# A gated recurrent stage: elementwise work moved off GpSimd, time-reversed value tiles moved one by one, and filling work re-spaced

## The chip, the cores and the metric

The kernel runs on one core of a Trainium2 chip. The core has TensorE (matrix products, PE in the profile), VectorE (DVE), ScalarE (ACT), GpSimd (POOL) and SyncE (SP, which only issues transfers), and 16 DMA engines. Each engine works through its own instructions strictly in order and waits on semaphores for the others. The metric is device microseconds of one execution; lower is better.

## The reference

One block of a hybrid model, batch 1, 1024 tokens, width 1024, fp32:

```python
h = rms_norm(x, norm1_gain)
hq, hf, hi, hg, sq, sk, sv, ga, gb = split_cols(h @ w_in, ...)
o_hg = hgrn2_mixer(hq, hf, hi, lower_bounds)              # recurrent stage, 8 heads of 128
o_hg = rms_norm(o_hg, hg_out_norm) * sigmoid(hg)
o_sb = stick_breaking(rms_norm(sq), rms_norm(sk), sv)     # attention stage, 16 heads of 64
x = x + (sigmoid(ga) * (o_hg @ w_hg_out) + sigmoid(gb) * (o_sb @ w_sb_out)) @ w_o
gate, up = split_cols(rms_norm(x, norm2_gain) @ w_ffn_in, ...)
x = x + (silu(gate) * up) @ w_ffn_out
```

The mixer works in chunks of 64 tokens. With `f = lb + (1 - lb) * sigmoid(hf)`, `k = 1 - f` and `c` the running sum of `log f` in the chunk:

```python
scores = einsum('td,tsd,sd->ts', q, exp(c[t] - c[s]) masked to s <= t, k)
o = scores @ v + (q * exp(c)) @ state
state = exp(c[last]) * state + (k * exp(c[last] - c)).T @ v
```

## The kernel before, in words

**Stages.** The order is: norm and transpose of x; projections of the forget and output gates of all heads (put into DRAM as `d_f` and `d_g`); the recurrent stage, head by head, some 190 to 555 us into the profile; the attention stage; the output projections; the feed-forward layer. Products of fp32 are made of three passes on a high part and a rest (`mm3`, lines 231 to 233). TensorE's order is exactly the order of the program text. The other engines' orders, and those of the DMA queues, are chosen by a scheduler from the program's order and its own idea of when each instruction is ready.

**Layout of a head.** Tokens lie in eight tiles of 128. Of each pair of tiles, the keys of the second are stored in reversed token order (`by_tile`, `odd`), so that a mask on scores can be shared; the values `v` of these tiles (index 1, 3, 5, 7) have to be reversed along their rows too. `hg_v` computes `v` for two heads at once (a pair of heads h, h + 1, h even), two token tiles per step `tp`. Line 560 copies the first of the two straight into `v`; line 557 copies the second into `vs`, which line 558 stores to DRAM (`d_v`). `turn_v` (line 564) then copies the whole pair's `d_v` with reversed rows to `d_vr` by a DMA issued from ScalarE's queue; `load_v` (line 568) loads `d_vr` into `v`, one DMA for each head of the pair, also from ScalarE's queue. For h > 0 the turn stands at the start of the pair's first `prep`, the load in its first step.

**A head's work.** `hg_gates(h)` makes `kv = 1 - f` and the running sum `c`. `prep` makes decayed keys and queries (`kb`, `qb`, `ke`, `qe`): subtraction, exponential on ScalarE, product. The tile of scores `sc` is cleared on GpSimd for every head. Then come 15 own steps: `base(0)` and `base(1)` (scores within 4 tokens, written into `sc` under a mask), `across` (scores between the halves of a tile), four `level`s (scores between blocks of 32, 16, 8 and 4 tokens; `level_prep` makes their operands), `turn` (transpose of `ke`, copied to `ket` by ScalarE, line 658), `state` (`ket` times `v`, line 667), `read` (`sc` times `v` and state times `qe`, lines 715 and 717) and `norm`. The first `state` step reads the token tiles 0 to 3, the second 4 to 6; tile 7 is read by `read(1)` alone. Of the operand buffers, `kb`, `qb` and the four levels' `kq` share four slots, and `ke`, `qe` and `sc` have one each; `kb`, `qb` and `ke` for the next head are made while this one runs.

**What stands on GpSimd.** `kv` (line 585), the clearing of `sc` (600), the subtraction for `qb` (604), for `ke` (614), the query half of `level_prep` (687), the last product of `norm` (729), and the DMAs that make the rest of a weight by accumulation (`rest_by_dma`, line 125).

**Filling.** Between own steps `weave` puts steps of other products: for head h the projection of q for head h + 1 (16 steps of three matmuls with 512 columns), then half of the `v` of a pair (32 steps of three matmuls with 256 columns); for heads 6 and 7 gate projections instead. Each own step has a number, each filling step too; after each own step, filling is put until

```python
pump(lead + (total - lead) * acc / span)
```

is reached, where `acc` is the sum of the own numbers so far and `span` their total. The numbers are weights for the order alone. An even head h also carries the first half of the v of pair h + 2, an odd head the second half of the v of pair h + 1.

**SyncE's queue** carries the weight loads (`wr`, line 136, two buffers), the loads of `fv` and `sg`, the stores of `d_v` and those of the head's output `d_ohg`. The program asks for them at the head's start in this order: the weights of the filling (`load_blocks`), then `prep`, then `hg_load` of the next head.

Of the kernel before, what the change touches and what calls it, by code (L numbers as in the profile page):

```python
# [7 lines left out]
F32 = mybir.dt.float32  # L8
# [3 lines left out]
AF = mybir.ActivationFunctionType  # L12
ALU = mybir.AluOpType
# [3 lines left out]
P = 128  # L17
S = 1024
D = 1024
KT = D // P  # L20
HS = 512
NT = S // P
# [19 lines left out]
def hybrid_block(ctx, tc, x, norm1_gain, w_in, lb_logits, hg_out_norm, sb_q_norm, sb_k_norm,  # L42
# [506 lines left out]
    def hg_v(h, tiles=range(4), get=None):  # L549
        get = get or in_block(2048 + h * P, 256)  # L550

        def evac(tp, ps):
            if tp == 0:
                for j in range(2):
                    hd[h + j]["v"] = hg.tile([P, NT, P], F32, tag="v", bufs=4, name="v")
            vs = hg.tile([P, 2 * P], F32, tag="vs", name="vs")
            nc.scalar.copy(vs, ps[:, 2 * P:])
            nc.sync.dma_start(d_v[h // 2, tp], vs)
            for j in range(2):
                nc.scalar.copy(hd[h + j]["v"][:, 2 * tp, :], ps[:, j * P:(j + 1) * P])  # L560
        return proj_v(get, evac, tiles)

    def turn_v(h):
        nc.scalar.dma_start(d_vr[h // 2], d_v[h // 2, :, ::-1, :])

    def load_v(h):
        for j in range(2):
            nc.scalar.dma_start(hd[h + j]["v"][:, 1::2, :],
                                d_vr[h // 2, :, :, j * P:(j + 1) * P].rearrange("a p c -> p a c"))

# [9 lines left out]
    def hg_gates(h):  # L580
        d = hd[h]
        fv = d["fv"]
        kv = d["kv"] = hg.tile([P, S], F32, tag="kv", name="kv")
        for dst, src in by_tile(kv, fv):
            nc.gpsimd.tensor_scalar(dst, src, -1.0, 1.0, op0=ALU.mult, op1=ALU.add)
        c = d["c"] = hg.tile([P, S], F32, tag="c", name="c")
        order(nc.scalar.activation(c, fv, AF.Ln, bias=tiny), *last["tables"])
        nc.vector.tensor_tensor_scan(c, rmask, c, initial=0.0, op0=ALU.mult, op1=ALU.add)

    def hg_head(h):  # L590
# [5 lines left out]
        def prep():  # L596
            if h % 2 == 0 and h > 0:
                turn_v(h)
            sc = e["sc"] = hg.tile([P, S], F32, tag="sc", bufs=1, name="sc")
            nc.gpsimd.memset(sc, 0.0)  # L600
            kb = e["kb"] = hg.tile([P, S], F32, tag="kl", bufs=4, name="kb")
            qb = e["qb"] = hg.tile([P, S], F32, tag="kl", bufs=4, name="qb")
            c4 = c.rearrange("p (b l) -> p b l", l=4)
            nc.gpsimd.tensor_sub(qb.rearrange("p (b l) -> p b l", l=4), c4,
                                 c4[:, :, 1:2].broadcast_to([P, S // 4, 4]))
# [6 lines left out]
            for dst, src in by_tile(ke, c):  # L612
                dst, src = (a.rearrange("p a (n c) -> p a n c", c=CH) for a in (dst, src))
                nc.gpsimd.tensor_sub(dst, src[:, :, :, CH - 1:CH].broadcast_to([P, NT // 2, 2, CH]), src)
            nc.scalar.activation(ke, ke, AF.Exp)
# [61 lines left out]
        def level_prep(li):  # L677
# [6 lines left out]
            for w, dst in enumerate(halves):  # L684
                src = pairs(c)[:, :, w, :].rearrange("p a (b two l) -> p a b two l", two=2, l=L)[:, :, :, 0, :]
                nc.vector.tensor_sub(dst, src[:, :, :, L - 1:L].broadcast_to([P, NT // 2, P // (2 * L), L]), src)
            nc.gpsimd.tensor_sub(qr, cl[:, :, 1, :], cl[:, :, 0, L - 1:L].broadcast_to([P, HS // L, L]))
            nc.scalar.activation(kq, kq, AF.Exp)
# [33 lines left out]
        def norm(half):  # L722
# [5 lines left out]
            nc.vector.scalar_tensor_tensor(r, po, cols[:, 32 + h:33 + h], r, op0=ALU.mult, op1=ALU.mult)  # L728
            nc.gpsimd.tensor_mul(r, r, sg[:, sl])
            nc.sync.dma_start(d_ohg[h][:, sl], r)  # L730

        return prep, [
            (0.86, lambda: (base(0), load_v(h) if h % 2 == 0 else None, level_prep(0),)),
            (2.46, lambda: (base(1), level_prep(1),)),
            (5.60, lambda: (across(), level_prep(2),)),
            (2.24, lambda: (level(0), level_prep(3),)),
            (0.50, lambda: (turn(0),)),
            (0.80, lambda: (turn(1),)),
            (0.85, lambda: (level(1),)),
            (1.85, lambda: (state(0),)),  # L740
            (0.70, lambda: (state(1),)),
            (0.61, lambda: (level(2),)),
            (3.99, lambda: (level(3),)),
            (1.60, lambda: (read(0),)),
            (4.50, lambda: (read(1),)),
            (2.97, lambda: (norm(0),)),
            (0.45, lambda: (norm(1),)),
        ]

# [52 lines left out]
    for n in range(n0):  # L802
        if n == n0 - 5:
            get = in_block(2048, 256)
            get()
            v0 = [hg_v(0, tiles, get) for tiles in ((0, 1), (2, 3))]
        weave([], pairs0.steps(n))
        if h_sums:
            h_sums.pop(0)()
    s0ctx.close()  # L810
    hg = hgctx.enter_context(tc.tile_pool(name="hg", bufs=2, reuse_waits="tile"))
    last["tables"] = [exp_ln_tables(last["sig0"])]
    hg_load(0)
# [4 lines left out]
    weave([], v0[1])  # L818
    turn_v(0)
    def urgent(steps):  # L820
# [5 lines left out]
    for h in range(NH):  # L826
# [12 lines left out]
        if h < NH - 1:  # L839
            hg_load(h + 1)  # L840
        weave(own, fill, lead=5.53)
    hgctx.close()
# [688 lines left out]
```

## Time and profile before

| | us |
|---|---|
| median of 3 runs (lowest, highest) | 2054.48 (2050.78, 2055.08) |
| the profiled execution: its own time | 2053.37 |
| the profiled execution: span from first to last instruction | 2051.3 |
| TensorE busy | 2006.9 |
| VectorE busy | 1522.5 |
| ScalarE busy | 1141.7 |
| GpSimd busy | 318.4 |
| `d_vr<-d_v`, share of the chain of waits over the whole span | 3% |

A row of a group reads: line, engine, operation, output <- inputs, shape, count, then busy us and mean ns of one, then the engine's idle time just before these instructions and what ended it. A row of a timeline gives start and length in us, with the idle time ahead of it and its releaser in brackets; "ACTq" and "SPq" are the issue of a DMA by that queue. A row of a table by stretch gives the stretch, its length, the busy time of PE, PEld, DVE, ACT and POOL with their counts of instructions, then the clock granted to TensorE as a share of full speed, the DMA engines' busy share and GB/s. A busy TensorE is not one at its peak, since the ends of matmuls are modelled and a lower clock lengthens them.

### The profile page before, as it was taken

What the parts mean: (1) busy time and instruction counts of PE and PEld (TensorE: products, weight loads), DVE (VectorE), ACT (ScalarE), POOL (GpSimd) and SP (SyncE); (2) the same over time, 40 slices, a digit from 0 to 9 for tenths busy, and PEclk for the clock granted to TensorE, in tenths of its full rate; (3) what the DMA queues carried; (4) which work ended last, traced back from release to release, by engine and by line L of the source; (5) the groups of instructions that cost most, each with busy time, mean ns of one, the idle gap of its engine ahead of it and who ended that gap; (6) DMA issues with size and microseconds to landing.
All of it is one profiled execution on the core that took longest, in us unless ns stands there. A gap on an engine that the chain in (4) does not pass through costs nothing.

```text
span 2051.3 us, 29673 instructions
## 1 busy us (share of the span) xinstructions
PE 2006.9 (98%) x10963; PEld 1720.6 (84%) x10963; DVE 1522.5 (74%) x2355; ACT 1141.7 (56%) x1957; POOL 318.4 (16%) x431
## 2 busy tenths in 40 slices
PE   8999899999999999999999999998999999999999
PEld 8888788898888988988988888887888888888887
DVE  7853777787367877787787598999766666668975
ACT  7544464555377777777777465547433333334443
POOL 0000444444222332332231000000000000000000
PEclk9999999999999999999999999999999999999999
DMA  5234446545455445455445646413323222256131
GB/s 184 98 114 144 128 120 158 144 114 152 117 117 125 89 107 118 99 118 121 101 105 120 216 147 210 166 35 111 102 74 105 78 72 77 78 203 222 42 113 41
DMA packets 209840, 245.23 MB, mean 120 GB/s; under 512 B 12008, under 2 KB 142496, under 8 KB 209696
## 3 DMA queue, kind: packets, MB, share of 16 engines
q1 hardware_dynamic: 188928, 202.84, 31.4%
q0 software_dynamic: 13616, 35.14, 10.3%
q10 hardware_dynamic: 7152, 5.37, 0.8%
q8 instruction: 86, 1.41, 0.3%
q14 instruction: 58, 0.48, 0.1%
HBM read 146.57 MB, written 51.12 MB: 96 GB/s over the span
## 4 chain that ended last, share of the span: by engine, by line
PE 71%; DVE 9%; DMA 4%; issue 2%; ACT 2%; POOL 1%; DVEq 0%; POOLq 0%; ACTq 0%
PE pd L231 14%; PE pd L232 14%; PE pd L233 14%; DMA d_vr<-d_v 3%; PE pt L1011 3%; PE pt L233 3%; PE pt L231 3%; PE pt L232 3%; PE po L1028 2%; PE po L231 2%; PE po L1027 2%; PE po L232 2%; PE po L233 2%; PE pz L966 2%; PE pz L967 2%
## 5 line engine op out<-in xcount | busy, mean ns | idle before, releaser
L167 ACT CAST wh<-u 128x512 fp32r<-128x512 f32 (+1 forms) x280 | 183.5, 684 | 224.9 <-PE po L233 86.6
L231 PE MATMUL pd<-hT,wh 128*128 128x512 f32 (+1 forms) x716 | 286.7, 400 | 0.0
L232 PE MATMUL pd<-hT,wh 128*128 128x512 f32 (+1 forms) x716 | 276.0, 385 | 0.5 <-DVE hT L281 0.5
L233 PE MATMUL pd<-hT,wl 128*128 128x512 f32 (+1 forms) x688 | 264.9, 385 | 0.0
L231 PE MATMUL pd<-u,wh 128*128 128x512 f32 x496 | 194.0, 391 | 1.5 <-ACT c L1394 0.7
L232 PE MATMUL pd<-u,wh 128*128 128x512 f32 x496 | 193.1, 389 | 0.2 <-DVE u L168 0.2
L168 DVE TENSOR_TENSOR wl<-u,wh 128x512 fp32r<-128x512 f32 (+1 forms) x196 | 150.5, 801 | 45.7 <-ACT wh L167 43.6
L231 PE MATMUL pd<-wh,hT 128*128 128x256 f32 x512 | 153.6, 300 | 0.0
L233 PEld LDWEIGHTS pd<-hT,wl 128*128 128x128 f32 x688 | 129.2, 188 | 26.9
L978 DVE TENSOR_TENSOR_SCAN kp<-kp,dsel 128x512 f32<-128x512 f32 (+3 forms) x128 | 123.5, 965 | 37.0 <-ACT kp L971 36.4
L232 PEld LDWEIGHTS pd<-hT,wh 128*128 128x128 f32 x716 | 135.2, 189 | 18.7 <-DVE hT L281 0.9
L231 PEld LDWEIGHTS pd<-hT,wh 128*128 128x128 f32 x716 | 135.0, 189 | 18.2
L232 PE MATMUL pd<-wl,hT 128*128 128x256 f32 x512 | 145.7, 285 | 2.7 <-DMA wl<-wr 1.7
L233 PE MATMUL pd<-wh,hT 128*128 128x256 f32 x512 | 145.6, 284 | 0.0
L971 ACT ACTIVATE kp<-pz,rq 128x128 f32<-128x128 f32 (+2 forms) x192 | 114.2, 595 | 43.9 <-PE pz L967 33.2
L233 PE MATMUL pd<-u,wh 128*128 128x512 f32 x352 | 137.0, 389 | 0.0
L164 DVE TENSOR_TENSOR u<-u,u 128x512 f32<-128x512 f32 (+1 forms) x152 | 124.7, 855 | 12.3 <-DMA u<-d_ohg 7.6
L1014 DVE TENSOR_TENSOR tl<-pt,th 128x512 fp32r<-128x512 f32 (+1 forms) x160 | 100.2, 627 | 33.5 <-ACT th L1013 33.1
L985 DVE TENSOR_TENSOR a<-a,kp 128x128 f32<-128x128 f32 (+2 forms) x192 | 109.7, 571 | 17.8 <-ACT a L971 3.4
L971 ACT ACTIVATE a<-pz,rq 128x128 f32<-128x128 f32 (+2 forms) x192 | 114.3, 595 | 7.0 <-PE pt L1011 7.0
L231 PEld LDWEIGHTS pd<-u,wh 128*128 128x128 f32 x496 | 93.1, 188 | 21.6 <-ACT c L1394 1.1
L232 PEld LDWEIGHTS pd<-u,wh 128*128 128x128 f32 x496 | 93.1, 188 | 19.8 <-DVE u L168 0.5
(305 smaller groups left out, 5293.5 us busy)
## 6 DMA issues: line engine op xcount, KB each, us to landing
wr<-in_w_in SPq DMA_DIRECT2D x72, 512.0 KB, 4.0
wl<-wr POOLq DMA_DIRECT2D x59, 512.0 KB, 4.9
u<-in_w_ffn_in SPq DMA_DIRECT2D x24, 512.0 KB, 4.7
wr<-in_w_ffn_in SPq DMA_DIRECT2D x20, 512.0 KB, 4.2
u<-in_w_ffn_out SPq DMA_DIRECT2D x10, 1024.0 KB, 6.7
d_act<-c SPq DMA_DIRECT2D x33, 256.0 KB, 2.1
u<-d_act SPq DMA_DIRECT2D x8, 1024.0 KB, 5.7
qh<-qh SPq DMA_DIRECT2D x48, 128.0 KB, 2.4
```

Of the source, the lines that this page charges most:

```text
L164: e.tensor_tensor(raw(to), raw(a), raw(b), op=op)
L167: nc.scalar.copy(hi, src)
L168: e.tensor_sub(lo, src, hi.bitcast(F32))
L231: nc.tensor.matmul(ps, lh, rh, start=start, stop=False, skip_group_check=adds)
L232: nc.tensor.matmul(ps, lh, rl, start=False, stop=False, skip_group_check=adds)
L233: nc.tensor.matmul(ps, ll, rh, start=False, stop=stop, skip_group_check=adds)
L966: nc.tensor.matmul(ps[:, :n], qhi[:, qs], kk[:, k0:k0 + n], start=True, stop=False)
L971: last["sig"] = [nc.scalar.activation(t[:, 0:w], ps[:, 0:w], AF.Sigmoid, scale=rq[:, n_, col:col + 1]) for n_, t in enumerate((kp, a))]
L978: nc.vector.tensor_tensor_scan(rev, rev, dsel[:, HS - w:][:, ::-1], initial=0.0, op0=ALU.mult, op1=ALU.max)
L985: nc.vector.tensor_mul(a[:, 0:w], a[:, 0:w], kp[:, 1:w + 1])
L1011: nc.tensor.transpose(tp[:, s * P:(s + 1) * P], a[:, b * P:(b + 1) * P], ident)
L1014: nc.vector.tensor_sub(tl[:, c0:], tp[:, c0:], th[:, c0:].bitcast(F32))
```

## The change

- The subtractions for `qb`, `ke` and the query half of each level, and the last product of `norm`, are done by VectorE; `kv` is made by ScalarE as `Identity(-1 * f + 1)`. GpSimd keeps the weight DMAs.
- `sc` is one tile for the whole stage, cleared once before the first head. Every head writes the same positions of it.
- `turn_v` turns one tile step `tp` of a pair, as two halves of 128 columns: rows of 512 bytes where there were rows of 1 KB. Tile step 0, 1 and 2 are turned when the values of the next step are copied out, tile step 3 after `base(1)` of the pair's first head. All four are issued by ScalarE's queue.
- `load_v` is issued by SyncE: tile steps 0 to 2 at the start of `prep` (for head 0 after the values are done), tile step 3 after `level(1)`. For each part there is one DMA for each head of the pair.
- The own steps' numbers and `lead` are others, so filling stands elsewhere.
- In the gate projections before the recurrent stage, four pieces of work on VectorE and ScalarE (`h_sums`) are asked for after the third to sixth product instead of the first to fourth.

```diff
@@ hg_v
+            if tp > 0:
+                turn_v(h, tp - 1)
@@
-    def turn_v(h):
-        nc.scalar.dma_start(d_vr[h // 2], d_v[h // 2, :, ::-1, :])
-
-    def load_v(h):
+    def turn_v(h, tp):
+        dst, src = (d[h // 2, tp].rearrange("p (j c) -> j p c", j=2) for d in (d_vr, d_v))
+        nc.scalar.dma_start(dst, src[:, ::-1, :])
+
+    def load_v(h, tiles):
         for j in range(2):
-            nc.scalar.dma_start(hd[h + j]["v"][:, 1::2, :],
-                                d_vr[h // 2, :, :, j * P:(j + 1) * P].rearrange("a p c -> p a c"))
+            nc.sync.dma_start(hd[h + j]["v"][:, 1 + 2 * tiles.start:2 * tiles.stop:2, :],
+                                d_vr[h // 2, tiles, :, j * P:(j + 1) * P].rearrange("a p c -> p a c"))
@@ hg_gates
-            nc.gpsimd.tensor_scalar(dst, src, -1.0, 1.0, op0=ALU.mult, op1=ALU.add)
+            nc.scalar.activation(dst, src, AF.Identity, scale=-1.0, bias=1.0)
@@ hg_head, prep
-                turn_v(h)
-            sc = e["sc"] = hg.tile([P, S], F32, tag="sc", bufs=1, name="sc")
-            nc.gpsimd.memset(sc, 0.0)
+                load_v(h, slice(0, 3))
+            e["sc"] = sc
@@
-            nc.gpsimd.tensor_sub(qb.rearrange("p (b l) -> p b l", l=4), c4,
+            nc.vector.tensor_sub(qb.rearrange("p (b l) -> p b l", l=4), c4,
@@
-                nc.gpsimd.tensor_sub(dst, src[:, :, :, CH - 1:CH].broadcast_to([P, NT // 2, 2, CH]), src)
+                nc.vector.tensor_sub(dst, src[:, :, :, CH - 1:CH].broadcast_to([P, NT // 2, 2, CH]), src)
@@ level_prep
-            nc.gpsimd.tensor_sub(qr, cl[:, :, 1, :], cl[:, :, 0, L - 1:L].broadcast_to([P, HS // L, L]))
+            nc.vector.tensor_sub(qr, cl[:, :, 1, :], cl[:, :, 0, L - 1:L].broadcast_to([P, HS // L, L]))
@@ norm
-            nc.gpsimd.tensor_mul(r, r, sg[:, sl])
+            nc.vector.tensor_mul(r, r, sg[:, sl])
@@ own steps
-            (0.86, lambda: (base(0), load_v(h) if h % 2 == 0 else None, level_prep(0),)),
-            (2.46, lambda: (base(1), level_prep(1),)),
-            (5.60, lambda: (across(), level_prep(2),)),
+            (1.53, lambda: (base(0), level_prep(0))),
+            (2.31, lambda: (base(1), turn_v(h, 3) if h % 2 == 0 else None, level_prep(1),)),
+            (3.27, lambda: (across(), level_prep(2),)),
             (2.24, lambda: (level(0), level_prep(3),)),
-            (0.50, lambda: (turn(0),)),
-            (0.80, lambda: (turn(1),)),
-            (0.85, lambda: (level(1),)),
-            (1.85, lambda: (state(0),)),
-            (0.70, lambda: (state(1),)),
-            (0.61, lambda: (level(2),)),
-            (3.99, lambda: (level(3),)),
-            (1.60, lambda: (read(0),)),
-            (4.50, lambda: (read(1),)),
+            (0.35, lambda: (turn(0),)),
+            (0.49, lambda: (turn(1),)),
+            (1.73, lambda: (level(1), load_v(h, slice(3, 4)) if h % 2 == 0 else None,)),
+            (1.28, lambda: (state(0),)),
+            (0.60, lambda: (state(1),)),
+            (0.64, lambda: (level(2),)),
+            (8.03, lambda: (level(3),)),
+            (1.04, lambda: (read(0),)),
+            (10.93, lambda: (read(1),)),
             (2.97, lambda: (norm(0),)),
-            (0.45, lambda: (norm(1),)),
+            (0.31, lambda: (norm(1),)),
@@ before the recurrent stage
-        if h_sums:
+        if h_sums and n > 1:
             h_sums.pop(0)()
     s0ctx.close()
     hg = hgctx.enter_context(tc.tile_pool(name="hg", bufs=2, reuse_waits="tile"))
+    sc = hg.tile([P, S], F32, bufs=1, name="sc")
+    nc.gpsimd.memset(sc, 0.0)
@@
-    turn_v(0)
+    load_v(0, slice(0, 3))
@@
-        weave(own, fill, lead=5.53)
+        weave(own, fill, lead=4.40)
```

## The prediction

> **What bounds the kernel now.** I read the page first, then the busy time head by head in the recurrent stage, then the waits of TensorE there, then the lines of time around the longest wait.
>
> ```profile
> span 2051.3 us, 29673 instructions
> PE 2006.9 (98%) x10963; PEld 1720.6 (84%) x10963; DVE 1522.5 (74%) x2355; ACT 1141.7 (56%) x1957; POOL 318.4 (16%) x431
> PE 71%; DVE 9%; DMA 4%; issue 2%; ACT 2%; POOL 1%; DVEq 0%; POOLq 0%; ACTq 0%
> ```
>
> TensorE is busy 98%, so only its idle 44 us, and time that it spends at a lower clock, can be won. Next come the stretches from one head's first base product to the next head's, for heads 0, 1, 2 and 4 (columns: PE, PEld, DVE, ACT, POOL busy, then the granted clock).
>
> ```profile
> 224.02:272.62 48.60, 38.34 (x264) 34.94 (x263) 31.39 (x50) 26.90 (x43) 17.57 (x17) 0.89 0.47 118
> 272.62:309.59 36.97, 35.91 (x264) 32.77 (x263) 28.02 (x48) 22.19 (x35) 18.81 (x15) 1.00 0.54 137
> 309.59:351.62 42.03, 37.64 (x264) 34.30 (x263) 31.88 (x48) 22.29 (x35) 16.29 (x16) 0.96 0.53 144
> 388.62:431.92 43.30, 38.96 (x265) 35.66 (x264) 31.86 (x48) 22.28 (x35) 16.30 (x15) 0.92 0.51 139
> ```
>
> All four run the same 264 or 265 matmuls. Odd head 1 takes 37.0 us at full clock, the even heads 48.6, 42.0 and 43.3 at a mean clock of 0.89 to 0.96: an even head, which begins a pair, has something that an odd one lacks. The waits of TensorE between 190 and 560 us say what (total, times, longest), and the clock where it dips:
>
> ```profile
> PE pt L667 <- ACT ket L658: 13.8, 5, 8.4
> PE pt L667 <- DMA v<-d_vr: 3.3, 4, 1.0
> PE pt L715 <- DVE sc L703: 2.5, 3, 1.1
> PE pd L232 <- DMA wl<-wr: 1.7, 2, 0.9
> PE pz L390 <- DVE sql L385: 1.3, 3, 0.4
> PE pd L232 <- ACT kq L688: 1.0, 1, 1.0
> ...
> 246.30:251.40 5.10, 4.64 (x20) 4.34 (x21) 1.34 (x4) 5.10 (x8) 0.91 (x1) 0.50 0.53 133
> 326.90:329.90 3.00, 3.00 (x14) 3.00 (x15) 1.21 (x4) 3.00 (x5) 0.90 (x1) 0.50 0.19 37
> 405.80:411.80 6.00, 5.95 (x28) 5.95 (x29) 2.38 (x7) 4.78 (x6) 0.91 (x1) 0.50 0.49 94
> ```
>
> Waits of 23.6 us, and 13.6 us of matmuls at half clock straight after the stalls of heads 0, 2 and 4, half of which (6.8 us) is lost. Where the 13.8 us come from, ScalarE's and TensorE's rows in head 2 show:
>
> ```profile
> 303.63 0.37 ACT L557 COPY vs<-pd 128x256 f32<-128x256 f32 x1
> 305.81 0.62 ACTq L564 DMA_DIRECT2D d_vr<-d_v  x1
> 323.78 0.93 ACTq L568 DMA_DIRECT2D v<-d_vr  x2
> 324.75 0.97 ACT L658 COPY ket<-pt 128x512 f32<-128x512 f32 x2 [7.48 <-DMA d_vr<-d_v]
> ...
> 323.05 0.28 PE L233 MATMUL pd<-wh,hT 128*128 128x256 f32 x1
> 325.39 0.49 PE L667 MATMUL pt<-v,ket 128*128 128x128 f32 x2 [2.07 <-ACT ket L658]
> 326.89 1.65 PE L667 MATMUL pt<-v,ket 128*128 128x128 f32 x6 [1.01 <-DMA v<-d_vr]
> ```
>
> The turn of the whole pair is issued at 305.81 and the loads at 323.78, 18.0 us later. ScalarE's queue stands on those loads until the turn has landed, so the ket copy behind them is late by 7.48 us, and then v itself lands another 3.1 us after its issue (326.89). Of the waits, those for ket, v, the weight rest `wl` (whose transfer runs beside the turn) and kq make 13.8 + 3.3 + 1.7 + 1.0 = 19.8; with the half clock 26.6 us: the **v group**. The other two, 2.5 + 1.3 = 3.8 us, are the **DVE group**.
>
> **The change part by part.** *Turn and load.* The loads leave ScalarE's queue, so the ket copy no longer stands behind them; whether TensorE gains depends on when v lands and when state(0) is due. By the weights of the old list (sum 29.98, lead 5.53, fill 20.96) the filling has given 16 steps of q and 7 of v before state(0); by the new one (sum 37.72, lead 4.40) the same 16 and none of v. Seven steps are 21 matmuls of 0.12 us, so state(0) comes 2.5 us sooner. Unstalled it would have come in head 2 at 323.2 less the 0.9 us wait for `wl`, so the new due time is 319.8. The last turned tile that it needs, tile 2, is issued with the copy of tile 3, near 303.9 instead of 305.81. Before shows no turn of one tile: a quarter of the whole is 4.5 us, the whole is 18.0. I take the middle, 11.3: 315.2, and 3.1 for the load, 318.3, 1.5 us before it is due. At the upper bound it is 325.0, a stall of 5.2. Head 0 is less lucky:
>
> ```profile
> 227.17 0.36 ACT L557 COPY vs<-pd 128x256 f32<-128x256 f32 x1
> 231.67 1.18 ACTq L564 DMA_DIRECT2D d_vr<-d_v  x1
> 244.66 0.94 ACTq L568 DMA_DIRECT2D v<-d_vr  x2
> ...
> 237.61 0.28 PE L233 MATMUL pd<-wh,hT 128*128 128x256 f32 x1
> 246.28 0.80 PE L667 MATMUL pt<-v,ket 128*128 128x128 f32 x2 [8.39 <-ACT ket L658]
> ```
>
> Due at 237.7 - 1.0 - 2.5 = 234.2. Issued at 227.5, half-way between 13.0 and 3.3 is 8.1, and 2.9 for the load (it lands by 247.54 there): 238.5, a stall of 4.3, with some 1 us of half clock behind it. So of the 26.6 us I keep 5.3 and win **21.3** (bounds 26.6, and about nothing at the upper ends). Tile 3 is read by read(1) alone, far behind; its turn waits on ScalarE's queue for a store that has landed by 305.8, where the old turn could go, and is asked for after base(1), past 311, so the scalar work behind it waits for nothing. The sixteen turns at 0.62 us of issue on ScalarE instead of four turns and eight loads are hidden: that engine is busy 22.3 of 42.0 us.
>
> *SyncE.* The loads go past this queue:
>
> ```profile
> 309.01 0.77 SPq L575 DMA_DIRECT2D sg<-d_g  x1
> 317.04 16.00 SPq L136 DMA_DIRECT2D wr<-in_w_in  x3
> SPq L136 <- DMA wl<-wr: 136.4, 24, 17.3
> ```
>
> SyncE stands 7 us before the first weight load of a head, waiting for a buffer, and issues three of them over 16 us. A load put ahead of these lets them wait for at most its turn (315.2, when they would wait to 317.0 anyway): nothing. `sg`, which the program asks for after the weights, already passes them, so I take it that what is ready first goes first. Put behind them, it is the slow rival below.
>
> *GpSimd's arithmetic.* On DVE the 128x1024 subtraction is priced by L610, each 128x512 one by L689's row alone, 0.68; kv on ScalarE by L607. Whether GpSimd costs DVE time now, the next rows say:
>
> ```profile
> 275.36 2.57 POOL L687 TENSOR_TENSOR kq<-c 128x512 f32<-128x512 f32 x2 [2.87 <-PE pz L628]
> 275.93 2.94 DVE L686 TENSOR_TENSOR kq<-c 128x256 f32<-128x256 f32 x4
> 280.00 0.68 DVE L689 TENSOR_TENSOR kq<-kq,q 128x512 f32<-128x512 f32 x1
> 295.89 1.43 DVE L686 TENSOR_TENSOR kq<-c 128x256 f32<-128x256 f32 x4
> L686 DVE TENSOR_TENSOR kq<-c 128x256 f32<-128x256 f32 x64 | 41.5, 702 | 0.0
> L689 DVE TENSOR_TENSOR kq<-kq,q 128x512 f32<-128x512 f32 x32 | 27.4, 857 | 1.8 <-ACT kq L688 1.6
> L610 DVE TENSOR_TENSOR qb<-qb,q 128x1024 f32<-128x1024 f32 x8 | 9.7, 1218 | 6.2 <-ACT qb L608 6.2
> L607 ACT ACTIVATE kb<-qb 128x512 f32<-128x512 f32 x16 | 9.1, 622 | 0.2 <-POOL qb L604 0.2
> ```
>
> Added to DVE: 8 x 1.22 + (16 + 32 + 16) x 0.68 = 53.3 us, 6.7 a head. Four subtractions take 2.94 us beside GpSimd's and 1.43 without, so L686 gives back 41.5 - 16 x 1.43 = 18.6 and L689 27.4 - 32 x 0.68 = 5.6: net 29 us, 3.6 a head. A pair of heads (28.0 + 31.9) would be at 67 of 72 us (twice TensorE's 35.9), 93% full. It lies beside TensorE's work, since most of it prepares the next head, but with less room. Bounds for what a fuller DVE costs: nothing; or, with no relief at all, 59.9 + 13.3 = 73.2 us a pair against 71.8, about 5 over the stage, and the old waits on top, 9. I take **+3.8**, as much again as the DVE group costs today. kv on ScalarE, 16 x 0.62, hides in its idle half.
>
> *Filling placed otherwise.* Ten steps of v instead of seven stand between level(3) and read(0), fourteen instead of seven between read(1) and norm(0): 1.1 and 2.5 us more against longest waits of 1.1 and 0.4. The DVE group's **3.8** goes (bounds 0 and 3.8).
>
> *Scores cleared once* and *h_sums two steps later*: the clear ran on GpSimd, and no wait of TensorE names it; the shift can move one wait before 190 us either way, by about 1 us. Both at nothing.
>
> Sum: 2051.3 - 21.3 - 3.8 + 3.8 = 2030.0 for the span. The profiled execution's own time is 2053.37, 2.1 more, which gives 2032.1; the median shown, 2054.48, is 1.1 above it: **2033**.
>
> **The rivals.** *Two engines for a turn.* If a turn's time goes by its count of pieces per engine rather than by bytes, a tile takes as long as the pair did: old, 4 tiles of 128 rows of 1 KB; new, 2 halves of 128 rows of 512 bytes. For it: the whole took 18 us for 512 KB, far from bandwidth. Against: it starts 1.9 us sooner, and its pieces are half the size. Then heads 2 and 4 stall 5.2 and head 0 stalls 227.5 + 13.0 + 2.9 - 234.2 = 9.2, with about 5 of half clock: some 25 of the 26.6 us stay, 2053; half-way between this and the forecast is 2043. The Trainium skill, DMA: Bandwidth & Descriptors, "Why a DMA increments its semaphore by 16 and not by 1", says that a transfer runs on the largest number of engines up to 16 that divides the slowest dimension of both sides; that would be 4 for the old turn and 2 for the new, and speaks against this edit. No view here names an engine; by that rule both turns have 128 pieces on each.
>
> *Loads behind the weights (slower).* If SyncE issues the load of tiles 0 to 2 behind all three weight loads, v lands at 333.0 + 3.1 = 336.1 against 319.8: a stall of 16.3 where 5 to 6 was lost before (42.0 and 43.3 against 37.0), so 10 more in each of heads 2, 4 and 6, less some 6 that head 0 wins: about +25, 2080. Behind the first alone (317.0) it costs 0.3; it decides from the second on (about 5, the old loss). For it: the program asks for the weights first. Against: `sg`'s row.
>
> *DVE sets the pace.* If GpSimd's relief doesn't come and every head pays a chain on DVE of 2 us more, 16 us of the 25 are eaten: 2045, inside the range.
>
> **How the numbers follow.** Forecast 0.55, its own range 2020 to 2041: below, v group and DVE group gone whole with nothing paid, 2054.5 - 30.4 = 2024, and some 4 more for fewer changes between filling and own work; above, DVE's 9 paid. Two engines 0.20 (2041 to 2054), DVE 0.10 (2041 to 2050), loads behind weights or a like wait on SyncE 0.15 (2058 to 2085). 2019 to 2052 leaves out the slow case and a little of the second. 0.2%, 4.1 us, is about what a measurement of this kernel can tell from no change. Faster: 0.55, 0.08 of DVE's and 0.13 of the second, 0.76; same 0.10; slower 0.14.
>
> **What would show it.** Right: ScalarE's ket copy waits for no d_vr; the waits of state's products fall from 17.1 to about 5 us, nearly all in head 0; the granted clock stays 1.00 in heads 2 and 4 and these take 36 to 38 us; four L686 subtractions take 1.4 us everywhere; DVE at about 31 to 33 us a head. Wrong: the wait for v stays above 4 us in heads 2 and 4 (two engines, or SyncE if its load is issued after a weight load); or waits of level and read products for DVE of more than 1 us a head.

## The result, and the profile after

| | before | after |
|---|---|---|
| median, us (lowest, highest; 4 runs each) | 2053.86 (2050.78, 2055.08) | 2025.10 (2024.29, 2025.95) |
| the profiled execution: its own time, its span | 2053.37, 2051.3 | 2025.34, 2023.5 |
| ratio after to before, 95% interval | | 0.9862 [0.9845, 0.9879] |

The changed kernel is faster by 28.8 us; 21 were forecast, and the time lies in the range. On another chip, beside the last three kernels below, the ratio was 0.9854 [0.984, 0.9867].

The page of the changed kernel, its busy times and its chain:

```profile
PE 1998.7 (99%) x10963; PEld 1716.7 (85%) x10963; DVE 1530.5 (76%) x2427; ACT 1152.9 (57%) x1973; POOL 201.4 (10%) x336
PE 77%; DVE 8%; issue 2%; ACT 1%; DMA 0%; POOL 0%; DVEq 0%; ACTq 0%; POOLq 0%
```

Transfers have gone from 4% of the chain to 0%. GpSimd has lost 117 us; VectorE has gained only 8 and ScalarE 11, though they took over its arithmetic: VectorE's own instructions became shorter.

The changed kernel's busy time by stretch, from one head's base(0) to the next head's, for heads 0, 1 and 2, and the sum of heads 0 to 6 (columns: PE, PEld, DVE, ACT, POOL, clock, DMA share, GB/s):

```profile
221.81:261.35 39.54, 37.39 (x264) 33.95 (x263) 34.90 (x61) 27.11 (x42) 2.19 (x3) 0.96 0.53 135
261.35:296.62 35.27, 35.27 (x264) 32.75 (x263) 31.32 (x57) 23.59 (x39) 2.52 (x4) 1.00 0.58 155
296.62:331.87 35.25, 35.25 (x264) 32.71 (x263) 31.29 (x56) 23.46 (x38) 2.62 (x4) 1.00 0.63 167
...
sum 250.59, PE 248.44 PEld 227.66 DVE 223.10 ACT 163.70 POOL 18.19; mean PE 35.49 PEld 32.52 DVE 31.87 ACT 23.39 POOL 2.60
```

The same sum for before:

```profile
sum 281.70, PE 258.21 PEld 233.66 DVE 209.50 ACT 156.33 POOL 119.54; mean PE 36.89 PEld 33.38 DVE 29.93 ACT 22.33 POOL 17.08
```

Every head from 1 on now has TensorE busy for its whole length, and even and odd heads are alike. Seven heads lose 281.70 - 250.59 = 31.1 us. Of these TensorE's idle time gives 23.5 - 2.2 = 21.3, and its busy time 258.21 - 248.44 = 9.8. Of the 9.8, half clock explains 5.1 (6.8 lost before, 1.7 after). The stage also begins 224.02 - 221.81 = 2.2 us sooner, mostly because the smaller lead puts less filling ahead of it: 1148 matmuls stand ahead of head 0's base(0) by the profile, 1155 in before; the seven come later. From head 7's base(0) to the end the span is longer: 1545.6 us (2051.3 less 224.02 and 281.70) became 1551.1, 5.5 more. So 31.1 + 2.2 - 5.5 = 27.8, the difference of the spans.

All waits of TensorE in the changed kernel between 190 and 560 us:

```profile
PE pz L704 <- DVE kq L694: 2.2, 1, 2.2
PE pz L913 <- POOL sq L892: 2.0, 1, 2.0
PE pz L913 <- POOL sq L891: 0.8, 1, 0.8
PE pt L1015 <- DVE a L989: 0.3, 1, 0.3
```

Waits of 23.6 us have become 5.3. The first is level(0) of head 0. The next two are new: they stand in the first norm of the attention stage, near 528 us, where before had no wait of TensorE at all from 506 to 560 us.

The turn and the load in head 2, from the changed kernel's timeline (ScalarE, then SyncE, then TensorE; L567 is the turn, L571 the load, L660 the ket copy, L669 the first state products):

```profile
289.69 0.57 ACTq L567 DMA_DIRECT2D d_vr<-d_v  x1
291.58 0.37 ACT L557 COPY vs<-pd 128x256 f32<-128x256 f32 x1 [0.58 <-PE pd L233]
305.74 0.97 ACT L660 COPY ket<-pt 128x512 f32<-128x512 f32 x2
...
294.85 0.91 SPq L571 DMA_DIRECT2D v<-d_vr  x2
...
305.52 3.57 SPq L136 DMA_DIRECT2D wr<-in_w_in  x2
...
307.30 1.05 PE L669 MATMUL pt<-v,ket 128*128 128x128 f32 x8
```

Tile 2's turn is issued at 289.69, ahead of tile 3's copy at 291.58. The load of tiles 0 to 2, which waits for it, is issued at 294.85, ahead of the weight loads, so the turn took at most 5.2 us. State needs `v` at 307.30, 12.4 us after the load's issue, and the ket copy waits for nothing.

### The profile page after: what moved, and what is told of

It reads as the page before. It is cut to its first block, busy times and chain, and to the rows that moved or that the text cites. A ratio compares the mean times of both kernels' runs of the same rounds, so it can differ in the third digit from the quotient of the medians.

```text
span 2023.5 us, 29581 instructions
## 1 busy us (share of the span) xinstructions
PE 1998.7 (99%) x10963; PEld 1716.7 (85%) x10963; DVE 1530.5 (76%) x2427; ACT 1152.9 (57%) x1973; POOL 201.4 (10%) x336
## 4 chain that ended last, share of the span: by engine, by line
PE 77%; DVE 8%; issue 2%; ACT 1%; DMA 0%; POOL 0%; DVEq 0%; ACTq 0%; POOLq 0%
PE pd L231 15%; PE pd L232 15%; PE pd L233 15%; PE pt L1015 3%; PE pt L233 3%; PE pt L231 3%; PE pt L232 3%; PE po L1032 2%; DVE u L164 2%; DVE u L168 2%; PE po L231 2%; PE po L232 2%; PE po L1031 2%; PE po L233 2%; PE pz L970 2%
```

## The experiments

Each ratio is against the kernel before on the same chip. The first four were run on one chip (before: 2056.67 us), the next four on another (2054.3), the last four on a third (2055.18).

**The new turn and load alone, in the kernel before** (turn_only). The edit is the change's own in these places; arithmetic, numbers and lead stay as before:

```diff
-    def turn_v(h):
-        nc.scalar.dma_start(d_vr[h // 2], d_v[h // 2, :, ::-1, :])
+    def turn_v(h, tp):
+        dst, src = (d[h // 2, tp].rearrange("p (j c) -> j p c", j=2) for d in (d_vr, d_v))
+        nc.scalar.dma_start(dst, src[:, ::-1, :])
...
-            (0.86, lambda: (base(0), load_v(h) if h % 2 == 0 else None, level_prep(0),)),
-            (2.46, lambda: (base(1), level_prep(1),)),
+            (0.86, lambda: (base(0), level_prep(0))),
+            (2.46, lambda: (base(1), turn_v(h, 3) if h % 2 == 0 else None, level_prep(1),)),
```

> The kernel before with the new turn and load alone (tile steps turned one by one, loads by SyncE, each at its new place); arithmetic on GpSimd, the clearing of the scores, the old numbers of the steps and h_sums stay. If the v group carries the gain: TensorE's waits of state's products (17.1 us) go below 3 us, the clock stays 1.00 in heads 2 and 4, and the time falls by 20 to 26 us, to 2028 to 2034. If the gain comes from GpSimd leaving VectorE's ports: the waits for v go, but others take their place, under 8 us of gain, 2046 or more. If the placing of the filling carries it: the same, 2046 or more.

Measured: 2040.82 us (2039.87 to 2043.11), ratio 0.9922 [0.9904, 0.994]: 15.9 us faster, between the forecasts (20 to 26, and under 8). Its two largest waits of TensorE between 190 and 560 us:

```profile
PE pt L718 <- DVE sc L706: 6.8, 7, 2.7
PE pz L705 <- DVE kq L695: 4.6, 3, 2.1
```

No wait for `v` or ket is left, so the turn does what the forecast said of it, and more. But waits for VectorE's `sc` and kq are now 11.4 us, where `sc` had 2.5 before and VectorE's kq none, and two stretches of half clock of 3.4 us each cost another 3.4. TensorE no longer stands still in the even heads, so the products there come sooner than VectorE, still slowed by GpSimd, has their operands. The timeline bears this out: of the 6.8 us for `sc`, the odd heads have 2.6, about what they had before, the even heads 4.2, where they had none, and the waits for kq stand in heads 0, 2 and 4.

**The changed kernel with the old turn and load** (old_turn), the reverse:

```diff
-            if tp > 0:
-                turn_v(h, tp - 1)
...
+    def turn_v(h):
+        nc.scalar.dma_start(d_vr[h // 2], d_v[h // 2, :, ::-1, :])
```

> The changed kernel with the old turn and load (whole pair turned by one transfer asked for in prep, loads by ScalarE in base(0)); arithmetic, the one clearing, numbers and h_sums as changed. If the v group carries the gain: state(0) is due 2.5 us sooner than before and ScalarE stands on the turn again, so 18 to 28 us come back, 2043 to 2053, with state's products waiting 15 us or more. If the ports or the filling carry it: it stays within 6 us of the changed kernel, 2031 or less.

Measured: 2054.88 us (2053.65 to 2058.12), ratio 0.9995 [0.9985, 1.0006]: the whole gain is gone. Its largest wait of TensorE:

```profile
PE pt L666 <- ACT ket L657: 19.1, 4, 6.0
```

This is 13.8 us before: with the arithmetic and the filling of the change, state is due sooner and waits longer for the same turn. The rest of the change does make the odd heads shorter (head 1 takes 35.25 us, 36.97 before), but the even heads give much of it back (head 2 takes 43.84, 42.03 before), so the seven heads take 278.1 us where they took 281.7. A new wait in the attention stage, told below, takes the remainder. So in the whole time the other edits gain nothing that can be measured while the wait for ket stands.

**The changed kernel with the arithmetic back on GpSimd** (pool_arith): five operations, of which

```diff
-            nc.vector.tensor_sub(qr, cl[:, :, 1, :], cl[:, :, 0, L - 1:L].broadcast_to([P, HS // L, L]))
+            nc.gpsimd.tensor_sub(qr, cl[:, :, 1, :], cl[:, :, 0, L - 1:L].broadcast_to([P, HS // L, L]))
```

is the query half of each level.

> The changed kernel with the five pieces of arithmetic back on GpSimd (kv, the subtractions for qb, ke and the levels, the last product of norm). Scores cleared once, the turn, the loads and the numbers as changed. If the v group carries the gain: 0 to 8 us come back, 2025 to 2033, as waits of level and read products for VectorE, with the four L688-like subtractions at 2.9 us beside GpSimd and 1.4 without. If the ports carry it: 15 us or more come back, 2040 or more.

Measured: 2047.77 us (2042.89 to 2051.81), ratio 0.9957 [0.9941, 0.9972]. In this company the arithmetic is worth 0.0095, about 19 us of the 28, far more than the forecast's terms for it; the figure is the rival's, 15 us or more. The wait of TensorE that carries it, the group of the four subtractions on VectorE, and head 2's timeline (VectorE, GpSimd, TensorE):

```profile
PE pt L659 <- DVE ke L645: 17.1, 6, 3.1
...
L688 DVE TENSOR_TENSOR kq<-c 128x256 f32<-128x256 f32 x60 | 59.2, 1041 | 0.0
...
306.48 7.28 DVE L688 TENSOR_TENSOR kq<-c 128x256 f32<-128x256 f32 x4
313.68 0.68 DVE L645 TENSOR_TENSOR ke<-ke,el 128x512 f32<-128x512 f32 x1
...
307.35 1.43 POOL L689 TENSOR_TENSOR kq<-c 128x512 f32<-128x512 f32 x1
309.06 1.89 POOL L689 TENSOR_TENSOR kq<-c 128x512 f32<-128x512 f32 x1
310.30 2.50 POOL L606 TENSOR_TENSOR qb<-c 128x1024 f32<-128x1024 f32 x1
...
314.41 1.15 PE L659 MATMUL pt<-ident,ke 128*128 128x128 f32 x7 [3.03 <-DVE ke L645]
```

Four subtractions that take 1.43 us alone last 7.28 us while GpSimd runs three of its own. The product for `ke` stands behind them in VectorE's queue, and turn(0), which the new numbers place sooner, waits 3.03 us for it. It is so in six heads. TensorE's waits between 190 and 560 us are 19.6 us in all, 14.3 more than in the change, and five stretches of half clock of 3.4 us stand there where the change has two. Each loses 1.7 us, so 14.3 + 3 x 1.7 = 19.4 accounts for the 19.

The same group in the changed kernel:

```profile
L688 DVE TENSOR_TENSOR kq<-c 128x256 f32<-128x256 f32 x60 | 22.8, 416 | 0.0
```

The mean of one is 416 ns without GpSimd's arithmetic, 702 before, and 1041 in this kernel. The Trainium skill, SBUF — State Buffer, "Who interferes with whom", says that a VectorE instruction with two inputs in SBUF contends with a GpSimd instruction that reads SBUF, and that the shared port pair behind this is an exclusive lock. The trace agrees: 7.28 us beside three GpSimd operations of 5.82 us in all is about the 1.43 us alone and the 5.82 one after the other.

**The changed kernel with the old numbers and lead** (old_fill):

```diff
-            (3.27, lambda: (across(), level_prep(2),)),
+            (5.60, lambda: (across(), level_prep(2),)),
...
-            (10.93, lambda: (read(1),)),
+            (4.50, lambda: (read(1),)),
...
-        weave(own, fill, lead=4.40)
+        weave(own, fill, lead=5.53)
```

> The changed kernel with the old numbers of the own steps and lead 5.53. If the numbers are worth the DVE group alone: 2 to 5 us come back, 2027 to 2030, as waits of read for the scores and of the norm sums. If the placing carries the gain: 15 us or more come back, 2040 or more.

Measured: 2041.53 us (2041.31 to 2042.0), ratio 0.9924 [0.9907, 0.9941]. Its largest wait of TensorE, and head 2's timeline (VectorE, TensorE):

```profile
PE pz L704 <- DVE kq L694: 9.0, 4, 2.4
...
312.42 1.29 DVE L616 TENSOR_TENSOR ke<-c 128x512 f32<-128x512 f32 x2 [0.97 <-PE pt L659]
313.63 0.69 DVE L691 TENSOR_TENSOR kq<-kq,q 128x512 f32<-128x512 f32 x1
314.23 0.75 DVE L694 TENSOR_TENSOR kq<-kq,kv 128x256 f32<-128x256 f32 x2
...
315.13 1.13 PE L704 MATMUL pz<-kq 128*128 128x128 f32 x8 [2.40 <-DVE kq L694]
```

Three of the four waits, 6.9 us, are level(1) in heads 2, 4 and 6; the fourth, 2.1 us, is level(0) of head 0, which waits in the change as well. With the old placing, VectorE does the next head's subtraction for `ke` (L616) first, stands 0.97 us for the transposes that must read the old `ke`, and makes level(1)'s operands last. Read products wait 2.8 us for the scores and norm sums 2.2, as forecast, but level(1) was not in the forecast. Together these 11.9 us are most of the 12.7 that come back (0.0062), which lies between the forecasts. The placing is worth that much only in this company. The four kernels that have the new turn:

| with the new turn | old filling | new filling |
|---|---|---|
| arithmetic on GpSimd | 0.9922 (turn_only) | 0.9957 (pool_arith) |
| arithmetic on VectorE | 0.9924 (old_fill) | 0.9862 (the change) |

In the whole time either edit alone gives nothing on top of the turn (the new filling alone costs 0.0035, 7 us); together they give 0.0060, 12 us. Both kernels in the lower row also pay some 4.5 us in the attention stage, as told below, which those in the upper row do not. Counted over the seven heads alone, where before takes 281.7 us, turn_only takes 268.5, pool_arith 275.7, old_fill 265.2 and the change 250.6: there the arithmetic alone gives 3.3 us, the new filling alone costs 7.1, and both together give 17.9. So the two help each other, and this does not rest on the attention stage. The table leaves out the clearing of `sc` and `h_sums`, which turn_only alone has as before; nothing separates these two.

**Before with the loads issued by SyncE, the turn as it was** (loads_sp):

```diff
-            nc.scalar.dma_start(hd[h + j]["v"][:, 1::2, :],
+            nc.sync.dma_start(hd[h + j]["v"][:, 1::2, :],
```

> The kernel before with one word changed: the two loads of v are issued by SyncE instead of ScalarE; the whole pair is still turned by one transfer asked for in prep. If ScalarE's standing on the loads is what TensorE pays for (the ket copy late by 7.5 us): the v group goes nearly whole, 2030 to 2036. If the late landing of the turn is: ket is in time, but v lands at the old place (or later, if SyncE issues the load behind a weight load) and TensorE waits for v instead, 2048 to 2056.

Measured: 2057.71 us (2053.71 to 2060.28), ratio 1.0011 [1.0002, 1.002]. Its largest wait of TensorE, and the ket copy in head 2:

```profile
PE pt L667 <- DMA v<-d_vr: 18.0, 4, 10.1
...
320.44 1.16 ACT L658 COPY ket<-pt 128x512 f32<-128x512 f32 x2 [2.33 <-PE pt L657]
```

The ket copy waits for its transposes alone, and TensorE waits as long as before, now for `v` itself. The queue that the ket copy stood in was not the limit; the landing of the turned values was.

**The change with the loads issued by ScalarE** (act_loads), the mirror:

```diff
-            nc.sync.dma_start(hd[h + j]["v"][:, 1 + 2 * tiles.start:2 * tiles.stop:2, :],
+            nc.scalar.dma_start(hd[h + j]["v"][:, 1 + 2 * tiles.start:2 * tiles.stop:2, :],
```

> The changed kernel with the loads of v issued by ScalarE again; tile by tile turns as changed. A turn of one tile lands about 5 us after its issue in the changed kernel, so ScalarE would stand at most that long, in a stretch with slack. If the landing is what counts: within 4 us of the changed kernel, 2023 to 2029. If the queue is: 10 us or more come back, 2035 or more.

Measured: 2027.27 us (2026.5 to 2027.95), ratio 0.9864 [0.9847, 0.988]. Against the change's 0.9862 the queue is worth nothing that can be measured, though a wait of 0.9 us for ket appears. The two runs together say the same from both sides: turning early and piece by piece is the gain, the queue is not. No run separates early from piece by piece. By the rows of head 2 the second is more: the turn was issued 6.9 us ahead of base(0) instead of 3.8, and took at most 5.2 us instead of 18.0.

**The change with a tile turned in four pieces of 64 columns instead of two of 128** (quarters):

```diff
-        dst, src = (d[h // 2, tp].rearrange("p (j c) -> j p c", j=2) for d in (d_vr, d_v))
+        dst, src = (d[h // 2, tp].rearrange("p (j c) -> j p c", j=4) for d in (d_vr, d_v))
```

> The changed kernel with each turn cut into four column pieces instead of two: 512 pieces of 256 bytes, slowest dimension 4. In the changed kernel one turn (256 pieces of 512 bytes) lands 5.2 us after its issue (289.69 to 294.85). If a turn's time goes by its bytes and a fixed part: the same 5 us. If by pieces over the engines that the slowest dimension allows (Trainium skill, DMA: Bandwidth & Descriptors, Why a DMA increments its semaphore by 16 and not by 1: 4 engines instead of 2, so 128 pieces on each as now): about the same or shorter by what half-size pieces save, 4 to 5 us. If pieces cost the same whatever the engines: 7 us or more. The whole time stays at 2025.

Measured: 2029.26 us in its one run, too few to tell 4 us from the forecast; no wait for `v`. Tile 2's turn and the load behind it, in the timeline of ScalarE and SyncE:

```profile
292.02 0.58 ACTq L567 DMA_DIRECT2D d_vr<-d_v  x1
...
296.13 0.90 SPq L571 DMA_DIRECT2D v<-d_vr  x2
```

At most 4.1 us from issue to the load, against 5.2 in the change. The profile names the turn as what SyncE waited for ahead of both loads. So pieces of equal cost whatever the engines (7 us or more) are ruled out; the other two cases, 5 us and 4 to 5, are too close to tell apart, and how the time of a turn is made up stays open. It does not matter for the result: state needs `v` 12.4 us after the load's issue in head 2, and both land in time.

**The wait in the attention stage, a first attempt** (split_lead). GpSimd splits q and k there into a cast and a remainder, in two halves; the edit holds the cast of half 1 behind the remainder of the half before, and gives head 0 a larger lead:

```diff
-        weave(own, fill, lead=4.40)
+        weave(own, fill, lead=4.40 if h else 7.00)
...
-                nc.gpsimd.tensor_copy(parts[:, i, :], sq)
-                nc.gpsimd.tensor_sub(parts[:, 2, :] if i else sq, sq, parts[:, i, :])
+                cast = nc.gpsimd.tensor_copy(parts[:, i, :], sq)
+                if i == 0 and "split" in last:
+                    order(cast, last["split"])
+                last["split"] = nc.gpsimd.tensor_sub(parts[:, 2, :] if i else sq, sq, parts[:, i, :])
```

> The changed kernel with its two remaining waits taken away: GpSimd's cast of the second half of the first attention queries is ordered behind the last subtraction of the first half (the old order), and the lead of head 0 alone is 7.00 instead of 4.40. The waits of 2.2 us (level, head 0) and 2.8 us (first q norm of the attention stage) go, and with them the two 3.4 us stretches of half clock behind them: 7 to 8.5 us, 2017 to 2019. If the order or the later base(0) puts another wait in their place: 2021 or more.

Measured: 2032.87 us (2031.88 to 2033.42), ratio 0.9891 [0.9876, 0.9906]: slower than the change. Its two largest waits of TensorE, and GpSimd's timeline:

```profile
PE pz L704 <- DVE kq L694: 4.5, 3, 3.0
PE pz L915 <- POOL sq L894: 3.6, 1, 3.6
...
535.56 0.91 POOL L125 DMA_DIRECT2D wl<-wr  x1 [5.94 <-ACT wl L124]
536.17 1.49 POOL L894 TENSOR_TENSOR sq<-sq,sq 128x512 bf16<-128x512 f32 x1
```

Freed from the cast, the scheduler put the transfer of a weight rest ahead of the remainder instead, and that transfer stood 5.94 us for ScalarE. The larger lead did not move level(0) away from VectorE's products either: its wait, now 3.0 us, is one of three.

The wait itself, in the timelines of GpSimd of the changed kernel and then of before:

```profile
526.57 1.17 POOL L891 CAST sq<-sq 128x512 bf16<-128x512 f32 x2 [4.75 <-ACT sq L889]
```

```profile
551.97 0.61 POOL L887 CAST sq<-sq 128x512 bf16<-128x512 f32 x1 [3.02 <-ACT sq L885]
552.66 1.17 POOL L888 TENSOR_TENSOR sq<-sq,sq 128x512 f32<-128x512 f32 x1
553.89 0.61 POOL L887 CAST sq<-sq 128x512 bf16<-128x512 f32 x1
```

No line of the change touches this place, but GpSimd's order here has changed with it. It now runs the casts of both halves together, so half 0's second part stands behind a cast that waits for ScalarE's half 1. In before, half 0 was done first. The new order comes with the arithmetic's move: old_turn and old_fill have these waits of 2.0 and 0.8 us too, pool_arith and turn_only, with the arithmetic on GpSimd, have none of them and run half 0 first.

The last four kernels follow from this. The changed kernel once more, to compare on one chip:

> The changed kernel once more, beside the next three on one chip. Theory: 2025 us within 2, a ratio of 0.986 within 0.0015; TensorE waits 2.2 us for kq ahead of level(0) of head 0 and 2.8 us for sq in the first norm of the attention stage, with 3.4 us at half clock behind each. Rival (the time found was a lucky chip): over 2030 us.

Measured: 2025.51 us (2023.70 to 2027.44), ratio 0.9854 [0.984, 0.9867], with the same waits of 2.1, 2.0 and 0.8 us.

**Both of GpSimd's other works held back** (split_both): the cast as above, and

```diff
+        if "parts" in last:
+            order(rest, last["parts"])
```

so that the next weight-rest transfer also stands behind the remainder.

> The changed kernel, with GpSimd's cast of half 1 and its next weight-rest transfers both held behind the last subtraction of the half before in the split of q and k of the attention stage. Theory (GpSimd's order there makes the new wait of the attention stage): the waits for sq of 2.0 and 0.8 us and the half clock behind them (3.4 us at half speed, 1.7 us lost) go: 4.5 us less than the changed kernel of the same chip, some 2021 us. Rival (the wait only moves, to the weight rests that now come later, as the earlier run with half of this edit had it): 0 to 6 us more than the changed kernel, with a wait of TensorE for wl or for sq.

Measured: 2020.88 us (2018.54 to 2022.51), ratio 0.983 [0.9817, 0.9843]: 4.6 us less than the changed kernel beside it, and the two ranges of times do not meet. Its largest wait of TensorE between 190 and 560 us:

```profile
PE pz L706 <- DVE kq L696: 2.2, 1, 2.2
```

This is head 0's level(0). The wait of the attention stage is gone, and the gain is the 4.5 us worked out. This version beats both kernels.

**Head 0's filling moved behind across(0)** (head0), so that level(0) comes later:

```diff
+        if h == 0:
+            own[1], own[2] = (0.2, own[1][1]), (9.0, own[2][1])
```

> The changed kernel, with the filling of head 0 placed behind the step across(0) rather than behind base(1), so that level(0) is due some steps later on TensorE. Theory (level(0) comes a fixed 2.2 us too soon behind the kq products of VectorE): the wait of 2.2 us and the 1.7 us lost to half clock go: 3.9 us less than the changed kernel of the same chip. Rival (the same gap opens ahead of across(0), which needs the same head's earlier products): no change within 1 us, with a wait of TensorE for VectorE ahead of across(0) in its place.

Measured: 2027.89 us (2026.78 to 2030.08), ratio 0.9866 [0.9853, 0.988]: no gain. Its waits in the recurrent stage:

```profile
PE pz L704 <- ACT c L590: 2.1, 1, 2.1
...
PE pz L704 <- DVE kq L694: 1.0, 1, 1.0
PE pt L669 <- ACT ket L660: 0.8, 1, 0.8
PE pt L717 <- DVE st L676: 0.8, 1, 0.8
```

With one more of 0.2 us for the scores, one wait of 2.2 us has become five of 4.9 in all: level(0) still waits for VectorE (1.0), level(1) of head 0 now waits as well (2.1; its release is put down to ScalarE's `c`, which ended last), and so do state in head 1 and read. Half clock no longer stands in the recurrent stage, but lasts 6.8 us instead of 3.4 in the attention stage. No wait stands ahead of across(0), so neither the theory nor its rival had the place. Moving the filling within the head only moves the wait.

**Both edits** (both_fixes):

> The two edits together. Theory: the two waits are independent, 190 to 530 us apart, so the gains add: 8.4 us less than the changed kernel of the same chip, some 2017 us. Rival: the sum of whatever the two single runs show, if one of them moves a wait rather than removing it.

Measured: 2022.66 us (2021.66 to 2024.62), ratio 0.984 [0.9826, 0.9853]: not better than split_both, whose times overlap with it. The rival's sum is what came: 4.6 less and 2.4 more make 2.2 less, and 2.9 less was measured.

## Why the prediction was right, and where its steps were off

The sign, the place and the main cause were right: the wait for the turned values bounded the stage, and the whole gain hangs on it (old_turn 0.9995), though the turn alone gives 15.9 us of it (turn_only). The steps one by one:

- *The v group, 26.6 us, of which 21.3 were to be won.* All of it went: the change has no wait for `v` or ket at all. The stall of 4.3 us in head 0 and the half clock behind it, which the forecast kept, did not come for `v`: `v` is asked for at 223.05 there, and state runs at 236.66. Two terms were mis-sized, the turn's time (11.3 us, the middle of 4.5 and 18.0; it took at most 5.2, near the lower bound) and its issue (put behind tile 3's copy; it came 1.9 us ahead of it). Rows of a transfer four times as large bounded the turn, and the middle was the cautious choice, not the one nearest in size. With it *two engines for a turn* fell: that rival needed 13 us or more.

```profile
223.05 1.37 SPq L571 DMA_DIRECT2D v<-d_vr  x2
...
236.66 1.05 PE L669 MATMUL pt<-v,ket 128*128 128x128 f32 x8
```

- *SyncE's queue: nothing.* Right. The load is issued ahead of the weight loads (294.85 against 305.52), and the slow rival, *loads behind the weights*, did not happen. The reason given was half of it: where the load is issued from matters little (act_loads), when the turn has landed matters.
- *When state is due.* 10.7 us after base(0) in head 2 (307.30 less 296.62), where the forecast had 319.8 less 309.59, 10.2.
- *GpSimd's arithmetic on VectorE.* The relief came as priced from the row of 1.43 us: each of the subtractions takes 404 to 430 ns, in every head, and VectorE is busy 31.3 us in heads 1 to 5, within the 31 to 33 named. *DVE sets the pace* did not come. But the sum had the move at +3.8, a cost, and pool_arith shows that without it 19 us come back: the step priced VectorE's own time and left out what its delays cost once TensorE no longer waits for `v`. The +3.8 for a fuller VectorE has its counterpart in head 0 alone: 2.2 us at level(0) and 1.7 of half clock, 3.9. The size agrees by luck. Ahead of that wait VectorE is busy without a break (3.41 of 3.41 us in the window shown at the end), while heads 1 to 6 show no wait at all.
- *Filling placed otherwise: -3.8.* The waits of the DVE group are gone. But the step failed in treating this edit and the arithmetic as separate terms that could be added. With the turn mended, the waits for `sc` and kq of VectorE grow from 2.5 to 11.4 us (turn_only), and it takes both edits to remove them. A sum over the waits seen in before could not hold them: while TensorE stood for `v`, VectorE caught up.
- *What the sum lacked.* The stage of seven heads gave 31.1 us. By the rows of waits and clock, what went in it is 23.6 of waits less head 0's 2.2, and 6.8 of half clock less 1.7: 26.5. The other 4.6 is matmul time outside half clock: the same matmuls are 4.7 us shorter in busy time. The runs trace most of it to the filling: with the old filling TensorE is busy 35.7 us in each of heads 1 to 5, though nothing waits for `v` (old_fill), with the new filling 35.25 in heads 1, 3 and 5 even with the old turn (old_turn), as in the change. These 0.45 us a head are some 3 of the 4.6. The forecast had them in its range, as some 4 us for fewer changes between filling and own work, and not in its sum. On the other side, 2.8 us of wait and 1.7 of half clock in the attention stage, 4.5 of the 5.5 us that the rest of the program lost, were not foreseen; split_both shows their cause. The forecast looked for the change's effects only in the stages that it edits. The median of 2025.1 us lies 8 us below the 2033 forecast; the range held, with the v group and the matmul time worth more than the sum had, and the attention stage taking part of it back.

## What to carry to other kernels

When one long wait covers a stage, take the waits behind it as unknown, not as the small numbers that the profile shows: price the edits that go with its removal together, and test them in pairs. Judge an engine that works beside the busy one by what the same instruction takes with and without its neighbour (416, 702 and 1041 ns here), since the neighbour's own busy time says nothing of it. Where a scheduler orders an engine's queue, look at the first work after the edited stage too; a fixed order of three instructions there was worth 4.6 us.

## What the runs showed of the hardware

Half clock does not follow from a wait's length. In the changed kernel 2.15 us of idle time ahead of level(0) were followed by 3.4 us at half clock, in old_fill 2.40 us ahead of level(1) by none. The difference is where the gap lies. In each profile that has several stretches of half clock, their starts lie whole multiples of 3.413 us apart; in the changed kernel 231.08 and 531.45, which is 88 of them. Cut along that grid, the changed kernel reads (busy time by stretch; PE comes first, the clock third from the end):

```profile
227.67:231.08 3.41, 1.26 (x9) 0.85 (x8) 3.41 (x9) 1.93 (x2) 0.00 (x0) 1.00 1.04 267
231.08:234.49 3.41, 3.41 (x12) 2.72 (x11) 3.04 (x8) 0.00 (x0) 0.00 (x0) 0.50 0.50 147
...
528.04:531.45 3.41, 1.44 (x20) 1.44 (x21) 0.17 (x1) 0.00 (x0) 3.41 (x5) 1.00 0.79 181
531.45:534.86 3.41, 3.41 (x19) 3.41 (x18) 0.00 (x0) 0.00 (x0) 1.08 (x1) 0.50 1.01 195
```

and old_fill, on its own grid, around its wait at 315.13:

```profile
310.41:313.82 3.41, 2.33 (x21) 2.12 (x19) 2.44 (x4) 1.97 (x3) 0.00 (x0) 1.00 0.65 208
313.82:317.24 3.42, 2.11 (x18) 2.14 (x19) 3.42 (x8) 1.99 (x4) 0.86 (x1) 1.00 0.25 54
317.24:320.65 3.41, 3.41 (x32) 3.41 (x31) 3.16 (x10) 3.41 (x7) 0.00 (x0) 1.00 0.61 115
```

A window in which TensorE is idle for 1.97 or 2.15 us is followed by one at half clock; a gap of 2.40 us that a boundary cuts into 1.08 and 1.31 costs nothing more. Cut along their own grids, the profiles of all 14 kernels agree, from 20 us after the start to 15 us before the end: of the windows at full clock, each one in which TensorE was idle for 1.95 us or more was followed by half clock, and none with 1.80 or less; the few between went both ways. So a wait of about 2 us costs its length and, by chance of its place on the grid, another 1.7 us. The Trainium skill, TensorE: Matmul & The Clock Gate, "What's actually happening", has the window of 3.4 us, free-running, and the grid agrees with it; it names an idle window as the condition, and here windows that were busy for 1.26 and 1.44 of 3.41 us were enough.
